# Attention of a hybrid encoder layer as a fixed-order pipeline, with the merge gates ahead of it and the softmax division moved to the outputs

## The chip, the cores and the metric

One core of one Trainium2 chip. The metric is the device time of one execution in microseconds, the median of several runs. The core has a matmul engine (PE, with its weight loads PEld), a vector engine (DVE), a scalar engine (ACT), a general engine (POOL, GpSimd) and a sequencer that issues most DMAs (SP). Each of them takes its instructions in the order in which they stand in its queue; they wait for each other through semaphores.

## The reference, cut to what matters

One layer is applied to two independent groups of 512 tokens (prompt and sample) with the same weights, all in float32. The part that is changed is latent attention with 8 heads, and the sigmoid merge gates that weigh both branches later.

```python
scale = (A_NOPE + A_ROPE) ** -0.5                       # (128 + 64) ** -0.5
qa = (rmsnorm(c_q, g_q) @ w_uq).reshape(B, S, A_HEADS, A_NOPE + A_ROPE)
q_nope, q_rope = qa[..., :A_NOPE], rope(qa[..., A_NOPE:], cos, sin)
kv = (rmsnorm(c_kv, g_kv) @ w_ukv).reshape(B, S, A_HEADS, A_NOPE + A_V)
k_nope, va = kv[..., :A_NOPE], kv[..., A_NOPE:]
k_rope = rope(k_r, cos, sin)                            # one key for all heads
s = q_nope . k_nope + q_rope . k_rope                   # per head, 512 x 512
p = softmax(s * scale)
y_a = (p @ va) @ w_ao
g_m, g_a = split(sigmoid(gm))                           # the merge gates, gm = h @ w
x = x + (g_m * y_m + g_a * y_a) @ w_out
```

## The kernel before

Tokens lie along the free axis, 512 to a tile (`T`), features along the 128 partitions; `g` is the group. A float32 product is made of three reduced-precision products: each operand is split into a high half (a cast to `float32r`, by ACT) and a low half (source minus high, `lo_of`, L153, by DVE, or by POOL for the values), and PE multiplies high by high, low by high and high by low. `split` (L156), `weight` (L163) and `proj1` (L175) do this for activations, weights and a projection.

The stages are: normalisation, the mLSTM heads with their chain, the merge gates, latent attention, two output projections by a scheme of seven products (`chain` and `Seven`), the last projection, the feed-forward part and an embedding. Around the change:

- `lat_norms` (L650) scales the latent vectors of q and kv by their inverse root mean squares.
- `merge_gate` (L684) projects one block of 128 gate channels for both groups: 48 matmuls, then a product and a tanh, and a store to DRAM. There are 16; `BULK` (L1426) says how many stand ahead of the value projection (10), after the first head's projections (2), and after heads 0 to 3 (1 each).
- The values of all heads are projected at L708 to L723 and stored to DRAM (`vd`).
- `attn_proj` (L762) makes the operands of one half-head, a head for one group: for even heads the rotary part of q for two heads (`rope`, L730, which reads the projection's bank in PSUM and shifts 32-partition blocks), then q and k, then loads the values and splits them.
- `attn` (L780) does, for each of four blocks of 128 queries: five score matmuls into a bank `sc`; row maximum (DVE, L794) and its negative times the scale; the exponential with the row sum (ACT, L797); the reciprocal; the rescaling of the probabilities `p` (ACT L800, or DVE L802 for block 1); four transposes on PE (L805) into a bank `pt`; the high half `aph` (ACT, L807) and the low half `apl` (DVE, L808). Then twelve matmuls weigh the values (L812 to L814), and the output goes to DRAM (`ozd`).
- `hops.need` (L867) prepares operands of the next stage (named P1, P2, P7, P6; P7 and P6 need a subtraction, on DVE and POOL), two or three after each half-head of heads 4 to 6 (`HOPS`, L1424).

What is not pinned is ordered by a planner, which simulates a timeline and can put instructions of one part between those of another; `pinned` (L65) makes all following instructions of DVE, ACT, PE and POOL, POOL's DMA issues included, keep the order of the program on their engine. In attention nothing is pinned. Banks in PSUM: two `pj`, three `sc`, two `pt`, one `av`.

Of the kernel before, what the change touches and what calls it, by code (L numbers as in the profile page):

```python
# [7 lines left out]
F32 = mybir.dt.float32  # L8
# [7 lines left out]
P = 128  # L16
# [46 lines left out]
def encoder_kernel(ctx: ExitStack, tc: tile.TileContext, a):  # L63
# [666 lines left out]
    def rope(src, nblk, by_dma=False):  # L730
        n = 32 * nblk
        r = Q("tr", "rp")
        V.tensor_tensor(out=r[0:n], in0=src[0:n], in1=cos[0:n], op=ALU.mult)
        s = Q("tr", "rs")
        m = EV("ch", "rm") if by_dma else None
        if by_dma:
            V.tensor_tensor(out=m, in0=src, in1=sin, op=ALU.mult)
        for i in range(nblk):
            f, o = slice(32 * i, 32 * i + 32), slice(32 * (i ^ 1), 32 * (i ^ 1) + 32)
            if by_dma:  # L740
                nc.sync.dma_start(s[o], m[f])
            else:
                V.tensor_tensor(out=s[o], in0=src[f], in1=sin[f], op=ALU.mult)
        V.tensor_tensor(out=r[0:n], in0=r[0:n], in1=s[0:n], op=ALU.add)
        return r

    kst = []
    for g in range(G):
        gs = Q("tr", "gs")
        nc.sync.dma_start(gs[0:64], gsd[g])  # L750
        r = rope(gs, 2)
        kh = Q.pool.tile([P, T], F32R, name=f"kh{g}")
        kl = Q.pool.tile([P, T], F32R, name=f"kl{g}")
        for o in (0, 64):
            S.copy(kh[o : o + 64], r[0:64])
        for o in (0, 64):
            V.tensor_tensor(out=kl[o : o + 64], in0=r[0:64], in1=kh[0:64].bitcast(F32), op=ALU.subtract)
        kst.append((kh, kl))
    scale = (128 + 64) ** -0.5
    qst = [[None] * 2 for _ in range(G)]  # L760

    def attn_proj(hd, g, wa):  # L762
        if hd % 2 == 0:
            r = rope(proj1(wa, lat["cq"][g], 2, 0, "pj"), 4, hd == 0)
            st0 = Q("qst", "qs0", F32R)
            st1 = Q("qst", "qs1", F32R)
            S.copy(st0[0:64], r[0:64])
            S.copy(st1[64:128], r[64:128])
            V.tensor_tensor(out=st0[64:128], in0=r[0:64], in1=st0[0:64].bitcast(F32), op=ALU.subtract)
            V.tensor_tensor(out=st1[0:64], in0=r[64:128], in1=st1[64:128].bitcast(F32), op=ALU.subtract)  # L770
            qst[g] = [st0, st1]
        qn = split(proj1(wa, lat["cq"][g], 2, 256, "pj"), Q, "qkv", "qn")
        kn = split(proj1(wa, lat["ckv"][g], 2, 512, "pj"), Q, "qkv", "kn")
        vt = Q("tr", "avt")
        c = hd % 4 * P
        nc.sync.dma_start(vt.rearrange("p (a b) -> p a b", a=NB), vd[g][hd // 4].rearrange("a p c -> p a c")[:, :, c : c + P])
        vn = split(vt, Q, "qkv", "vn", GP)
        return qn, kn, vn, qst[g][hd % 2]

    def attn(hd, g, ops):  # L780
        (qh, ql), (nh, nl), (vh, vl), q2 = ops
        kh, kl = kst[g]
        ph = Q("ph", "aph", F32R, (P, NB, T))
        pl = Q("pl", "apl", F32R, (P, NB, T))
        for i in range(NB):
            c = slice(i * P, (i + 1) * P)
            bk = bank("sc")
            E.matmul(bk, qh[:, c], nh, start=True, stop=False)
            E.matmul(bk, qh[:, c], nl, start=False, stop=False)
            E.matmul(bk, ql[:, c], nh, start=False, stop=False)  # L790
            E.matmul(bk, q2[:, c], kh, start=False, stop=False)
            E.matmul(bk, q2[:, c], kl, start=False, stop=True)
            mx = sm.tile([P, 4], F32, name=nm("mx"), tag="mx", bufs=4)
            V.tensor_reduce(out=mx[:, 0:1], in_=bk, axis=mybir.AxisListType.X, op=ALU.max)  # L794
            V.tensor_scalar(out=mx[:, 1:2], in0=mx[:, 0:1], scalar1=-scale, scalar2=None, op0=ALU.mult)
            p = Q("p", "p")
            S.activation(out=p, in_=bk, func=AF.Exp, bias=mx[:, 1:2], scale=scale, accum_out=mx[:, 2:3])  # L797
            V.reciprocal(out=mx[:, 3:4], in_=mx[:, 2:3])
            if i != 1:
                S.activation(out=p, in_=p, func=AF.Copy, scale=mx[:, 3:4])  # L800
            else:
                V.tensor_scalar(out=p, in0=p, scalar1=mx[:, 3:4], scalar2=None, op0=ALU.mult)  # L802
            tp = bank("pt")
            for j in range(NB):
                E.transpose(tp[:, j * P : (j + 1) * P], p[:, j * P : (j + 1) * P], ident)  # L805
            tp3 = tp.rearrange("p (a b) -> p a b", a=NB)
            S.copy(ph[:, :, c], tp3)  # L807
            lo_of(pl[:, :, c], tp3, ph[:, :, c])  # L808
        ob = bank("av")
# [227 lines left out]
    wa = weight(a["wa"][0])  # L1037
    ops = [attn_proj(0, g, wa) for g in range(G)]
    for _ in range(BULK[1]):
        merge_gate(*bulk.pop(0))  # L1040
    for hd in range(AH):
        if hd < AH - 1:
            wa = weight(a["wa"][hd + 1])
        else:
            QL.close()
            X2 = Slots("X2", "right", x=16)
            assert not units
            hops.r, hops.t = {}, {}
            hops.raw = lambda g, k: load(hzd[g][k], X2, "x")
        for g in range(G):  # L1050
            attn(hd, g, ops[g])
            if hd < AH - 1:
                ops[g] = attn_proj(hd + 1, g, wa)
            for _ in range(HOPS.get((hd, g), 0)):
                hops.need(*units.pop(0))
        for _ in range(BULK[2 + hd]):
            merge_gate(*bulk.pop(0))
# [461 lines left out]
```

## Time and profile before

| | us |
|---|---|
| median of 3 runs | 1871.39 (1870.98 to 1872.51) |
| the profiled execution | 1872.55 |
| its span | 1870.8 |
| merge gates and value projection, from about 484 to 561 | 77 |
| attention, from about 561 to 848 | 287 |

Durations come from the profiled execution; the span is from its first to its last instruction, and 1.75 us lie around it. Times in a view are from the span's start. A name such as `apl<-pt,aph` means that tile `apl` is written from `pt` and `aph`; buffer numbers are left out.

### The profile page before, as it was taken

The page shows a single profiled execution, that of the slowest core. Times are in us where ns is not written, and L with a number is a line of the kernel's source. Part 1 is how long each engine was busy: PE and PEld are TensorE (multiplying, and loading weights), DVE is VectorE, ACT ScalarE, POOL GpSimd, SP SyncE. Part 2 cuts the span into 40 slices and gives each one's busy share as a digit, 9 for nine tenths or more (in the row PEclk, how much of TensorE's full clock was granted, in tenths as well). Part 3 has the DMA queues.
Part 4 walks back from the last instruction along what each step waited for, and adds up shares of the span by engine and source line. Part 5 has one row for each costly group of instructions (what it writes and reads, how often), then busy time and mean ns, then how long its engine had stood idle before and what let it go on. Part 6 is the DMA issues. An engine that isn't in the chain of part 4 may idle for free.

```text
span 1870.8 us, 24407 instructions
## 1 busy us (share of the span) xinstructions
PE 1831.6 (98%) x8801; PEld 1524.5 (81%) x8801; DVE 1244.1 (67%) x2196; ACT 890.1 (48%) x1725; POOL 385.8 (21%) x281
## 2 busy tenths in 40 slices
PE   9999999999999999899999999999999999999997
PEld 7889898988887888678878888887888877888786
DVE  6767575767616757976997586444444469878656
ACT  6255555653334656784543364333333343534333
POOL 0101010100000001241230005654666423111000
PEclk9999999999999999999999999999999999999998
DMA  4211212122443113345564332322233256533332
GB/s 166 66 57 52 67 47 79 35 74 79 141 155 107 65 63 117 109 146 210 181 205 155 117 141 74 124 96 96 91 106 119 96 169 209 168 126 103 105 130 96
DMA packets 100617, 212.40 MB, mean 114 GB/s; under 512 B 10960, under 2 KB 21584, under 8 KB 100496
## 3 DMA queue, kind: packets, MB, share of 16 engines
q1 hardware_dynamic: 87840, 166.01, 26.2%
q10 hardware_dynamic: 12096, 43.00, 6.8%
q8 instruction: 69, 1.13, 0.2%
q0 software_dynamic: 560, 1.84, 0.2%
q14 instruction: 52, 0.43, 0.1%
HBM read 156.05 MB, written 54.23 MB: 112 GB/s over the span
## 4 chain that ended last, share of the span: by engine, by line
PE 84%; DVE 9%; DMA 3%; ACT 2%; issue 1%; SPq 0%; ACTq 0%; DVEq 0%
PE b L945 12%; PE b L947 12%; PE b L946 12%; PE mm L183 8%; PE mm L185 8%; PE mm L184 8%; PE mm L79 3%; PE nm L622 3%; DVE xl L154 2%; PE mm L542 2%; PE mm L541 2%; PE mm L540 2%; DVE wp L154 1%; PE pt L805 1%; PE mm L1311 1%
## 5 line engine op out<-in xcount | busy, mean ns | idle before, releaser
L946 PE MATMUL b<-xl,wp 128*128 128x512 f32 x1148 | 448.3, 392 | 1.8 <-DVE xl L154 1.8
L945 PE MATMUL b<-xh,wp 128*128 128x512 f32 x1148 | 442.1, 393 | 6.9 <-ACT u L986 2.3
L947 PE MATMUL b<-xh,wp 128*128 128x512 f32 x1148 | 444.0, 392 | 1.8 <-DVE wp L154 1.8
L889 ACT CAST wp<-wst 128x512 fp32r<-128x512 f32 (+1 forms) x270 | 164.3, 612 | 307.4 <-PE b L947 259.9
L154 DVE TENSOR_TENSOR wp<-wst,wp 128x512 fp32r<-128x512 f32 (+1 forms) x270 | 234.3, 870 | 65.8 <-ACT wp L889 65.7
L945 PEld LDWEIGHTS b<-xh,wp 128*128 128x128 f32 x1148 | 216.0, 188 | 59.6 <-ACT wp L889 5.7
L947 PEld LDWEIGHTS b<-xh,wp 128*128 128x128 f32 x1148 | 216.0, 188 | 49.7 <-DVE wp L154 2.7
L946 PEld LDWEIGHTS b<-xl,wp 128*128 128x128 f32 x1148 | 215.9, 188 | 49.1 <-DVE xl L154 2.7
L183 PE MATMUL mm<-hh,whi 128*128 128x512 f32 x560 | 219.7, 392 | 0.2 <-DVE qnl L154 0.2
L184 PE MATMUL mm<-hl,whi 128*128 128x512 f32 x560 | 218.6, 390 | 0.0
L185 PE MATMUL mm<-hh,wlo 128*128 128x512 f32 x560 | 218.5, 391 | 0.0
L991 DVE TENSOR_TENSOR u<-b,u 128x512 f32<-128x512 f32 x90 | 61.6, 688 | 132.4 <-PE b L947 82.6
L185 PEld LDWEIGHTS mm<-hh,wlo 128*128 128x128 f32 x560 | 105.2, 188 | 21.9 <-DVE wlo L154 0.3
L183 PEld LDWEIGHTS mm<-hh,whi 128*128 128x128 f32 x560 | 105.2, 188 | 21.7 <-DVE qnl L154 0.7
L168 ACT CAST whi<-wst 128x1024 fp32r<-128x1024 f32 (+1 forms) x69 | 70.7, 1025 | 108.5 <-PE mm L184 67.7
L184 PEld LDWEIGHTS mm<-hl,whi 128*128 128x128 f32 x560 | 105.2, 188 | 21.0
L916 POOL TENSOR_TENSOR s<-wst,wst 128x512 f32<-128x512 f32 (+1 forms) x30 | 48.2, 1606 | 323.3 <-DMA wst<-w 148.0
L154 DVE TENSOR_TENSOR wlo<-wst,whi 128x1024 fp32r<-128x1024 f32 (+1 forms) x69 | 83.9, 1216 | 34.6 <-ACT whi L168 33.8
L986 ACT COPY u<-b 128x512 f32<-128x512 f32 x90 | 50.8, 589 | 97.8 <-PE b L947 72.2
L1209 POOL TENSOR_TENSOR sg<-sg,u 128x512 f32<-128x512 f32 x30 | 55.0, 1833 | 203.6 <-DVE u L991 203.6
L154 DVE TENSOR_TENSOR xl<-ld,xh 128x512 fp32r<-128x512 f32 x121 | 90.0, 771 | 5.6 <-ACT xh L873 4.9
L154 POOL TENSOR_TENSOR vnl<-avt,vnh 128x512 fp32r<-128x512 f32 x16 | 21.2, 1322 | 344.1 <-ACT vnh L158 285.7
(346 smaller groups left out, 3601.1 us busy)
## 6 DMA issues: line engine op xcount, KB each, us to landing
wst<-w SPq DMA_DIRECT2D x73, 512.0 KB, 3.3
wst<-w ACTq DMA_DIRECT2D x60, 512.0 KB, 3.4
ld<-actd SPq DMA_DIRECT2D x77, 256.0 KB, 3.9
actd<-t SPq DMA_DIRECT2D x40, 256.0 KB, 3.0
x<-x SPq DMA_DIRECT2D x32, 256.0 KB, 4.7
ld<-hzd SPq DMA_DIRECT2D x32, 256.0 KB, 2.8
wst<-wd ACTq DMA_DIRECT2D x16, 512.0 KB, 3.5
actd<-sg SPq DMA_DIRECT2D x30, 256.0 KB, 2.1
```

What stands on the lines that cost most here:

```text
L79: r = f(*args, **kw)
L154: e.tensor_tensor(out=out, in0=src, in1=hi.bitcast(F32), op=ALU.subtract)
L168: S.copy(hi[:, :n], st[:, :n])
L183: E.matmul(bk, whi[:, c], hi, start=k == 0, stop=False)
L184: E.matmul(bk, whi[:, c], lo, start=False, stop=False)
L185: last_mm[0] = E.matmul(bk, wlo[:, c], hi, start=False, stop=k == nk - 1)
L622: E.matmul(bk, l, r, start=n == 0, stop=n == len(terms) - 1)
L889: S.copy(hi, src)
L945: E.matmul(bk, whi[:, c], hi, start=bool(first) and k == 0, stop=False, **sk)
L946: E.matmul(bk, whi[:, c], lo, start=False, stop=False, **sk)
L947: E.matmul(bk, wlo[:, c], hi, start=False, stop=k == self.kh - 1, **sk)
L991: V.tensor_tensor(out=t, in0=b, in1=t, op=ALU.add if name == "P2" else ALU.subtract)
```

## The change

All 16 merge gates stand ahead of the value projection (`BULK = [16]`). The scale of the scores goes into q's normalisation. Attention becomes a loop over `u`, the 16 half-heads, pinned from its first to its last instruction, in which the steps of half-head `u`, of the one before and of the one after are written in one order; `m` is `u // 4` (two heads, both groups) and `r` is `u % 4`. The probabilities stay undivided. The reciprocals of the row sums are transposed, stored to DRAM and loaded back as a row on all partitions (both DMAs issued by POOL), and POOL multiplies the output by that row. The rotary steps work on a copy of the projection in SBUF (tag `rt` in `AX`) and are spread over several half-heads, as are the splits of the weights. `WX`, the weight tiles of the next stage, is opened after half-head 12. The scores' matmul with q's low half comes last of its five. The products with the probabilities' low halves come last of the twelve.

```diff
@@ lat_norms
-            V.tensor_tensor(out=r[:, c], in0=r[:, c], in1=rcol[g], op=ALU.mult)
+            V.scalar_tensor_tensor(
+                out=r[:, c], in0=r[:, c], scalar=SCALE if n == "cq" else 1.0, in1=rcol[g], op0=ALU.mult, op1=ALU.mult
+            )
@@ tiles
-    Q = Slots("Q", tr=3, qkv=12, qst=4, p=3, ph=1, pl=1)
+    Q = Slots("Q", vt=2, rb=1, qkv=12, qst=4, p=3, ph=1, pl=1)
-    WX = Slots("WX", "right", wst=2, s3=2, wp=1)
+    AX = Slots("AX", "right", rt=4)
@@ new functions in place of rope, attn_proj and attn
+    def rope_steps(t, s, nblk):
+        n = 32 * nblk
+        for i in range(nblk):
+            f, o = slice(32 * i, 32 * i + 32), slice(32 * (i ^ 1), 32 * (i ^ 1) + 32)
+            yield V.tensor_tensor(out=s[o], in0=t[f], in1=sin[f], op=ALU.mult)
+        yield V.tensor_tensor(out=t[0:n], in0=t[0:n], in1=cos[0:n], op=ALU.mult)
+        yield V.tensor_tensor(out=t[0:n], in0=t[0:n], in1=s[0:n], op=ALU.add)
...
+    def wa_split(hd):
+        w = was[hd] = [WP(n, n, F32R, (P, 1024)) for n in ("whi", "wlo")]
+        st = wload[hd]
+        for c in (slice(256, 768), slice(0, 256)):
+            if c.start == 256 or hd in (0, 1, 3, 5):
+                S.copy(w[0][:, c], st[:, c])
+                lo_of(w[1][:, c], st[:, c], w[0][:, c])
+    def rot_proj(m, g):
+        t = rots[m, g] = AX("rt", "rp")
+        S.copy(t, proj1(was[max(2 * m - 1, 0)], lat["cq"][g], 2, 0, "pj"))
+        rsteps[m, g] = rope_steps(t, AX("rt", "rs"), 4)
...
+    def score(u, i):
...
+        E.matmul(bk, qn[u][0][:, c], kn[u][0], start=True, stop=False)
+        E.matmul(bk, qn[u][0][:, c], kn[u][1], start=False, stop=False)
+        E.matmul(bk, q2[:, c], kst[g][0], start=False, stop=False)
+        E.matmul(bk, q2[:, c], kst[g][1], start=False, stop=False)
+        E.matmul(bk, qn[u][1][:, c], kn[u][0], start=False, stop=True)
+        V.tensor_reduce(out=x["mx"][:, i : i + 1], in_=bk, axis=mybir.AxisListType.X, op=ALU.max, negate=True)
...
+    def sums_row(u):
...
+        E.transpose(tp[0:NB, 0:P], x["rc"], ident)
+        rb = x["rb"] = Q("rb", "rb")
+        S.copy(rb[0:NB, 0:P], tp[0:NB, 0:P])
+        GP.dma_start(rsd[g][hd], rb[0:NB, 0:P])
+        GP.dma_start(rb, rsd[g][hd].rearrange("a p -> (a p)")[None, :].to_broadcast([P, T]))
...
+    def weighed(u):
...
+        S.copy(o, x["ob"])
+        GP.tensor_tensor(out=o, in0=o, in1=x["rb"], op=ALU.mult)
         nc.sync.dma_start(ozd[g][hd], o)
@@ the loop, in place of that over heads and groups
+    def hop_hi(n, k):
+        src = hops.part(n, k)
+        hi, lo = op(n, "xh", F32R), op(n, "xl", F32R)
+        S.copy(hi, src)
...
+    pinned[0] = True
+    for u in range(NU + 1):
+        now, then, nxt = u < NU, u > 0, u + 1 < NU
+        m, r = u // 4, u % 4
+        if now:
+            score(u, 0)
+            expo(u, 0)
+            score(u, 1)
...
+        if then:
+            turn(u - 1, 3)
+        if now:
+            expo(u, 1)
+        if then:
+            V.reciprocal(out=att[u - 1]["rc"], in_=att[u - 1]["den"])
+            turn_lo(u - 1, 3)
+        if nxt:
+            proj_hi(kn, u + 1, "ckv", 512)
+            proj_lo(kn, u + 1)
+        if now:
+            vn[u] = [Q("qkv", n, F32R) for n in ("vh", "vl")]
+            S.copy(vn[u][0], vts[u])
+            lo_of(vn[u][1], vts[u], vn[u][0], GP)
+        if then:
+            sums_row(u - 1)
+        los = []
+        if now and r:
+            for n in (("P1", "P2"), ("P7",), ("P6",))[r - 1]:
+                los.append(hop_hi(n, m))
...
+        if r == 0 and 0 < m < 4:
+            rot_hi(m, 1)
+            rot_lo(m, 1)
+        if m < 3:
+            if r == 0:
+                rot(m + 1, 0, 2)
+            if r == 1:
+                rot(m + 1, 0, 4)
+            if r == 2:
+                rot(m + 1, 1, 4)
+            if r == 3:
+                rot(m + 1, 1, 2)
+                rot_hi(m + 1, 0)
+                rot_lo(m + 1, 0)
+        if then:
+            weigh(u - 1)
+            weighed(u - 1)
+        if now:
+            turn(u, 0)
+            turn_lo(u, 0)
+            score(u, 2)
+            turn(u, 1)
+            expo(u, 2)
+            turn_lo(u, 1)
+        if r == 1 and m < 3:
+            wa_split(2 * m + 2)
+        if r == 3 and m < 3:
+            wa_split(2 * m + 3)
+        for x in los:
+            lo_of(*x)
+        if nxt:
+            proj_hi(qn, u + 1, "cq", 256)
+        if now:
+            score(u, 3)
+        if nxt:
+            proj_lo(qn, u + 1)
+        if now:
+            turn(u, 2)
+            expo(u, 3)
+            turn_lo(u, 2)
+        if r == 0 and m < 3:
+            rot_proj(m + 1, 1)
+        if r == 3 and m < 2:
+            rot_proj(m + 2, 0)
...
-BULK = [10, 2, 1, 1, 1, 1, 0, 0, 0, 0]
+BULK = [16]
```

`turn` transposes one block of probabilities and casts the high half, `turn_lo` makes the low half; `rot` runs some of the rotary steps, `rot_hi` and `rot_lo` split their result; `proj_hi` and `proj_lo` project and split k or q; `weigh` is the twelve value matmuls.

More of the change, by code (lines that the diff above doesn't have):

```diff
@@ L724, in encoder_kernel @@
     ozd = [[dr.tile([P, T], F32, name=f"ozd{g}_{c}") for c in range(AH)] for g in range(G)]
+    rsd = [[dr.tile([NB, P], F32, name=f"rsd{g}_{c}") for c in range(AH)] for g in range(G)]
     cos = Q.pool.tile([P, T], F32, name="cos")
@@ L728, in encoder_kernel @@
     nc.sync.dma_start(sin, a["sin"])
-    def rope(src, nblk, by_dma=False):
+    def rope_steps(t, s, nblk):
         n = 32 * nblk
[L732 to L737, printed above, removed]
         for i in range(nblk):
             f, o = slice(32 * i, 32 * i + 32), slice(32 * (i ^ 1), 32 * (i ^ 1) + 32)
[L740 to L745, printed above, removed]
+            yield V.tensor_tensor(out=s[o], in0=t[f], in1=sin[f], op=ALU.mult)
+        yield V.tensor_tensor(out=t[0:n], in0=t[0:n], in1=cos[0:n], op=ALU.mult)
+        yield V.tensor_tensor(out=t[0:n], in0=t[0:n], in1=s[0:n], op=ALU.add)
     kst = []
     for g in range(G):
-        gs = Q("tr", "gs")
+        gs = AX("rt", "gs")
         nc.sync.dma_start(gs[0:64], gsd[g])
-        r = rope(gs, 2)
+        for _ in rope_steps(gs, AX("rt", "rs"), 2):
+            pass
         kh = Q.pool.tile([P, T], F32R, name=f"kh{g}")
@@ L754, in encoder_kernel @@
         for o in (0, 64):
-            S.copy(kh[o : o + 64], r[0:64])
+            S.copy(kh[o : o + 64], gs[0:64])
         for o in (0, 64):
-            V.tensor_tensor(out=kl[o : o + 64], in0=r[0:64], in1=kh[0:64].bitcast(F32), op=ALU.subtract)
+            V.tensor_tensor(out=kl[o : o + 64], in0=gs[0:64], in1=kh[0:64].bitcast(F32), op=ALU.subtract)
         kst.append((kh, kl))
[L759 to L774, printed above, removed]
+    halves_ = [(hd, g) for hd in range(AH) for g in range(G)]
@@ new lines, in encoder_kernel, with wa_load @@
+    NU = len(halves_)
+    was, wload, qn, kn, vn, vts, rots, rsteps, qst, att = ({} for _ in range(10))
+    def wa_load(hd):
+        wload[hd] = WP("wst", "wst", F32, (P, 1024))
+        nc.sync.dma_start(wload[hd][:, 0:768], a["wa"][hd])
+    def wa_split(hd):
[5 more added lines that the diff above has]
+                lo_of(w[1][:, c], st[:, c], w[0][:, c])
@@ new lines, in rot_proj, with rot, rot_hi @@
+    def rot_proj(m, g):
+        t = rots[m, g] = AX("rt", "rp")
+        S.copy(t, proj1(was[max(2 * m - 1, 0)], lat["cq"][g], 2, 0, "pj"))
+        rsteps[m, g] = rope_steps(t, AX("rt", "rs"), 4)
+    def rot(m, g, n):
+        for _ in range(n):
+            next(rsteps[m, g])
+    def rot_hi(m, g):
+        t = rots[m, g]
+        qst[m, g] = st = [Q("qst", "qs", F32R) for _ in range(2)]
+        for i in range(2):
+            f = slice(64 * i, 64 * i + 64)
+            S.copy(st[i][f], t[f])
@@ new lines, in rot_lo, with proj_hi, proj_lo @@
+    def rot_lo(m, g):
+        t, st = rots[m, g], qst[m, g]
+        for i in range(2):
+            f, o = slice(64 * i, 64 * i + 64), slice(64 - 64 * i, 128 - 64 * i)
+            V.tensor_tensor(out=st[i][o], in0=t[f], in1=st[i][f].bitcast(F32), op=ALU.subtract)
+    def proj_hi(to, u, n, off):
+        hd, g = halves_[u]
+        bk = proj1(was[hd], lat[n][g], 2, off, "pj")
+        hi = Q("qkv", "qh", F32R)
+        S.copy(hi, bk)
+        to[u] = (hi, Q("qkv", "ql", F32R), bk)
+    def proj_lo(to, u):
+        hi, lo, bk = to[u]
+        lo_of(lo, bk, hi)
@@ L775, in attn_proj, with v_load @@
+    def v_load(u):
+        hd, g = halves_[u]
+        vt = vts[u] = Q("vt", "avt")
         c = hd % 4 * P
         nc.sync.dma_start(vt.rearrange("p (a b) -> p a b", a=NB), vd[g][hd // 4].rearrange("a p c -> p a c")[:, :, c : c + P])
[L777 to L809, printed above, removed]
@@ new lines, in score @@
+    def score(u, i):
+        hd, g = halves_[u]
+        if i == 0:
+            att[u] = dict(
+                mx=sm.tile([P, NB], F32, name=nm("mx"), tag="mx", bufs=2),
+                den=sm.tile([P, NB], F32, name=nm("den"), tag="den", bufs=2),
+                rc=sm.tile([P, NB], F32, name=nm("rc4"), tag="rc4", bufs=1),
+                bk={}, p={}, tp={},
+            )
+        x, c, q2 = att[u], slice(i * P, (i + 1) * P), qst[hd // 2, g][hd % 2]
+        bk = x["bk"][i] = bank("sc")
+        E.matmul(bk, qn[u][0][:, c], kn[u][0], start=True, stop=False)
[4 more added lines that the diff above has]
+        V.tensor_reduce(out=x["mx"][:, i : i + 1], in_=bk, axis=mybir.AxisListType.X, op=ALU.max, negate=True)
@@ new lines, in expo, with turn @@
+    def expo(u, i):
+        x = att[u]
+        p = x["p"][i] = Q("p", "p")
+        S.activation(
+            out=p, in_=x["bk"][i], func=AF.Exp, bias=x["mx"][:, i : i + 1], accum_out=x["den"][:, i : i + 1]
+        )
+    def turn(u, i):
+        x = att[u]
+        if i == 0:
+            x["ph"] = Q("ph", "aph", F32R, (P, NB, T))
+            x["pl"] = Q("pl", "apl", F32R, (P, NB, T))
+        tp = bank("pt")
+        for j in range(NB):
+            E.transpose(tp[:, j * P : (j + 1) * P], x["p"][i][:, j * P : (j + 1) * P], ident)
+        x["tp"][i] = tp.rearrange("p (a b) -> p a b", a=NB)
+        S.copy(x["ph"][:, :, i * P : (i + 1) * P], x["tp"][i])
@@ L810, in attn, with weigh @@
+    def weigh(u):
+        x, (vh, vl) = att[u], vn[u]
+        ob = x["ob"] = bank("av")
         for j in range(NB):
             c = slice(j * P, (j + 1) * P)
-            E.matmul(ob, vh[:, c], ph[:, j], start=j == 0, stop=False)
-            E.matmul(ob, vl[:, c], ph[:, j], start=False, stop=False)
-            E.matmul(ob, vh[:, c], pl[:, j], start=False, stop=j == NB - 1)
+            E.matmul(ob, vh[:, c], x["ph"][:, j], start=j == 0, stop=False)
+            E.matmul(ob, vl[:, c], x["ph"][:, j], start=False, stop=False)
+        for j in range(NB):
+            E.matmul(ob, vh[:, j * P : (j + 1) * P], x["pl"][:, j], start=False, stop=j == NB - 1)
@@ L815, in attn @@
+    def weighed(u):
+        hd, g = halves_[u]
+        x = att[u]
         o = EV("ch", "oz")
-        S.copy(o, ob)
+        S.copy(o, x["ob"])
+        GP.tensor_tensor(out=o, in0=o, in1=x["rb"], op=ALU.mult)
         nc.sync.dma_start(ozd[g][hd], o)
@@ L1018, in encoder_kernel @@
     hops.tmp = lambda: None
-    units = [(n, [k]) for k in range(4) for n in ("P1", "P2", "P7", "P6")]
     z1d = [[dr.tile([P, T], F32, name=f"z1d{g}_{c}") for c in range(KD)] for g in range(G)]
@@ L1035, in pair @@
         return ops, lambda: Seven(srcs, 4, ops, outputs(put), e)
[L1037 to L1044, printed above, removed]
+    for hd in range(2):
+        wa_load(hd)
+        wa_split(hd)
+    v_load(0)
+    for g in range(G):
+        rot_proj(0, g)
+        rot(0, g, 6)
+        rot_hi(0, g)
+        rot_lo(0, g)
@@ new lines, in encoder_kernel, with hop_load @@
+    for to, n, off in ((kn, "ckv", 512), (qn, "cq", 256)):
+        proj_hi(to, 0, n, off)
+        proj_lo(to, 0)
+    rot_proj(1, 0)
+    def hop_load(k):
+        for x in "acbd":
+            hops.get(x, k)
+    def hop_hi(n, k):
+        src = hops.part(n, k)
+        hi, lo = op(n, "xh", F32R), op(n, "xl", F32R)
+        S.copy(hi, src)
+        hops.x.setdefault(n, []).append((hi, lo))
+        return lo, src, hi
+    hop_load(0)
+    pinned[0] = True
[7 more added lines that the diff above has]
+        if nxt:
+            v_load(u + 1)
+            if r == 0 and m < 3:
+                wa_load(2 * m + 2)
+            if r == 2 and m < 3:
+                wa_load(2 * m + 3)
+        if then:
[19 more added lines that the diff above has]
+            if r == 3 and m < 3:
+                hop_load(m + 1)
+        if r == 0 and 0 < m < 4:
[24 more added lines that the diff above has]
+            wa_split(2 * m + 2)
+        if r == 3 and m < 3:
+            wa_split(2 * m + 3)
[5 more added lines that the diff above has]
+            score(u, 3)
+        if nxt:
+            proj_lo(qn, u + 1)
[3 more added lines that the diff above has]
+            turn_lo(u, 2)
+        if r == 0 and m < 3:
+            rot_proj(m + 1, 1)
+        if r == 3 and m < 2:
+            rot_proj(m + 2, 0)
+        if u == 12:
+            AX.close()
+            WX = Slots("WX", "right", wst=2, s3=2, wp=1)
+        if u == NU - 2:
@@ L1045, in encoder_kernel @@
             QL.close()
             X2 = Slots("X2", "right", x=16)
[L1047 to L1057, printed above, removed]
+    pinned[0] = False
@@ L1058, in encoder_kernel @@
+    hops.r, hops.t = {}, {}
+    hops.raw = lambda g, k: load(hzd[g][k], X2, "x")
     assert not bulk
@@ L1467, in _layout @@
     for hd in range(AH):
-        wa[hd, :, 0:256] = rq[hd // 2]
+        wa[hd, :, 0:256] = rq[min((hd + 1) // 2, AH // 2 - 1)]
         wa[hd, :, 256:512] = uq[hd]
```

8 lines of the change are left out of this document (7 added, 1 removed).

## The prediction, made before the changed kernel ran

> **What bounds the kernel now.** The page first, for who is busy; then windows, to see where that breaks down.
>
> ```profile
> span 1870.8 us, 24407 instructions
> ...
> PE 1831.6 (98%) x8801; PEld 1524.5 (81%) x8801; DVE 1244.1 (67%) x2196; ACT 890.1 (48%) x1725; POOL 385.8 (21%) x281
> ```
>
> PE is busy 98%, but the ends of matmuls are modelled, so I count instructions instead. Windows of all instructions, windows of those on `pt` alone (the transposes), and a line of the chain that ended last:
>
> ```profile
> 484.00:557.00 73.00, 73.00 (x327) 60.39 (x326) 29.64 (x40) 27.11 (x42) 0.00 (x0) 1.00 0.47 160
> ...
> 557.00:736.00 179.00, 178.42 (x845) 146.51 (x845) 113.98 (x228) 103.42 (x200) 12.11 (x9) 1.00 0.26 85
> 736.00:848.00 112.00, 101.31 (x483) 79.54 (x482) 88.99 (x186) 83.44 (x174) 39.18 (x30) 0.98 0.40 128
> ...
> 557.00:736.00 179.00, 18.83 (x128) 15.69 (x128) 21.80 (x32) 18.58 (x32) 1.00 0.26 85
> 736.00:848.00 112.00, 19.52 (x128) 15.52 (x128) 21.95 (x32) 19.12 (x32) 0.98 0.40 128
> ...
> 597.42 0.87 PE pt L805 x8
> ```
>
> Columns of a window: its length, then busy time and count of PE, PEld, DVE, ACT, POOL, then PE's granted clock. From 484 to 557 gates and v projection issue 319 matmuls and 8 transposes without a gap: a transpose takes 0.87 / 8 = 0.109 us, a 512-wide matmul (73.0 - 0.87) / 319 = 0.226. At that rate 557 to 736 needs 717 x 0.226 + 128 x 0.109 = 176.0 of its 179.0, and 736 to 848 needs 355 x 0.226 + 14.0 = 94.2 of 112.0. Attention loses 3.0 us while merge gates (48 matmuls, 10.9 us each) fill it, and 17.8 without them: **20.8 us is all that a better order can win here**, and elsewhere nothing is touched.
>
> **The change part by part.** *Gates.* Six move ahead of attention, 65 us there instead of here, at the full rate of 484 to 557, where DVE (29.6 of 73) and ACT (27.1) leave them room: price 0. What goes is the filler.
>
> *Small parts.* Sixteen transposes of the sums: 16 x 0.109 = 1.7 us more PE. In `lat_norms` one instruction becomes another: 0. Weights and values are loaded by SP a unit ahead: 0, and a late load would cost at most its landing. The next stage's weight tiles (WX) exist only from the 13th unit on; three units, some 36 us, remain to load them: 0.
>
> *The pipeline.* With 16 half-heads ("units") and no filler, all depends on whether four in-order engines keep step. The durations:
>
> ```profile
> 598.65 0.69 ACT L797 ACTIVATE p<-sc,mx 128x512 f32<-128x512 f32 x1
> 599.24 0.20 ACT L797 ACTIVATION_READ_ACCUMULATOR p<-sc,mx 128x1 f32 x1
> 599.33 0.63 ACT L688 ACTIVATE tg<-tg 128x512 f32<-128x512 f32 x1
> 599.85 0.59 ACT L807 CAST aph<-pt 128x512 fp32r<-128x512 f32 x1
> 600.32 0.61 ACT L158 CAST qnh<-pj 128x512 fp32r<-128x512 f32 x1
> ...
> 574.09 1.28 DVE L794 TENSOR_REDUCE mx<-sc 128x1 f32<-128x512 f32 x2
> ...
> 570.95 0.69 DVE L769 TENSOR_TENSOR qs<-rp,qs 64x512 fp32r<-64x512 f32 x1
> 571.67 1.78 DVE L770 TENSOR_TENSOR qs<-rp,qs 64x512 fp32r<-64x512 f32 x1
> ...
> 571.61 1.30 POOL L154 TENSOR_TENSOR vnl<-avt,vnh 128x512 fp32r<-128x512 f32 x1 [158.20 <-ACT vnh L158]
> ...
> 763.00 0.68 DVE L743 TENSOR_TENSOR rs<-pj,sin 32x512 f32<-32x512 f32 x1
> 763.71 0.69 DVE L154 TENSOR_TENSOR apl<-pt,aph 128x512 fp32r<-128x512 f32 x1
> ...
> 763.23 1.29 POOL L917 TENSOR_TENSOR wst<-wst 128x512 f32<-128x512 f32 x1
> ```
>
> From start to start: an exponential 0.68, a copy from PSUM 0.47 (from SBUF I take 0.52); a DVE instruction 1.28 - 0.68 = 0.60, one that shifts partitions (`qs`, rotary) 0.71. And a coupling: `qs` at 571.67 takes two SBUF tiles and needs 1.78, ending 0.5 after POOL's `vnl` ends at 572.9, while `rs` and `apl`, which read PSUM, run at 0.68 beside POOL's add at 763.23. So a DVE instruction on two SBUF tiles waits for POOL's. Before, the rotary products read `pj` in PSUM; now they read its copy in SBUF, behind kn's low half, just when POOL splits the values: 1.3 us lost in most units.
>
> Need per unit on PE: 20 score, 12 projection, 12 value matmuls and 17 transposes, 11.84 us; with a rotary projection 13.2. By these rates DVE needs 8.9 to 10.5 and ACT 8 to 9, so no engine but PE is full. The loss comes from the order. I walk it from the start of a unit's first score, with 0.06 us from a release to a start and 0.2 for a weight load that was held.
>
> **Second unit of a group of four.** DVE: two maxima to 3.2, low half of the last probabilities 4.3 (after ACT's copy), kn's 5.6, four rotary instructions from 6.8 (behind POOL) to 9.5, two low halves and a maximum to 11.4. Then the weights' low half, which waits for ACT's high half (after the third exponential) until 12.3; two low halves of the next stage's operands (P1, P2) to 14.1; only then the fourth maximum, 14.7, and q's low half, 15.3. PE wants that for the fifth matmul of the next unit's first score at about 13.2: late by 2.3, and the third unit's third exponential makes PE's T2 late by about 1 more. The third unit of a group so loses 3.5, three times.
>
> **Fourth unit.** POOL's order is: values, store of the sums' reciprocals to DRAM, broadcast load back, P6's subtraction, product. The load must wait for the store's landing on POOL's own queue, and behind it stands P6; ACT waits for P6, and behind that on ACT stand the rotary copies, the output's copy, two probability copies and the third exponential, for which PE waits. Prices of a store from POOL:
>
> ```profile
> 1563.05 0.54 POOL L1220 DMA_DIRECT2D actd<-t  x1 [1.26 <-DVE t L1216]
> ...
> actd<-sg SPq DMA_DIRECT2D x6, 256.0 KB, 2.0
> ...
> actd<-sg POOLq DMA_DIRECT2D x3, 256.0 KB, 4.6
> ...
> 59.64 2.36 DMA lfd<-lf
> ...
> DMA to landing us min/median/max: 3.2/3.4/3.6
> ```
>
> A 256 KB store from POOL lands after 4.6, from SP 2.0; a small one from SP (`lfd`) 2.36. This small one from POOL lies between 2.0 and 4.6; I take 3.0, nearer to `lfd` by size. The broadcast (16 such by SP, `b<-nmd`, 3.4) holds only the product behind it. Sum: values end 7.0, store landed 10.0, load issued 10.6, P6 done 11.9, ACT's copy 12.0 instead of 5.9; then 0.52 + 2 x 0.52 + 3 x 0.48, the third maximum, the exponential, and PE's T2 starts at 17.1 instead of 11.7: 5.4, of which 2.0 to 4.6 for the landing makes 4.4 to 7.0. Behind T2 the rotary projection waits 1.2 for its weights, split after that exponential. So 6.8, 6.8, 5.7, 6.9 in the four groups.
>
> [...]
>
> *Ends.* First unit 2.3 (no previous unit's work between its scores and its transposes); second units 0.5 each, last group's third 0.4, first units 0.6, 0.6, 1.7; draining the last unit 2.7. Head: from split weights to the first score the chain is projection 1.4, copy 0.6, six rotary instructions 4.1, copies 1.1, low halves 1.4, in all 8.6 with hops, against 30 projection matmuls (6.8 us), of which some wait too: I take 3, between 0 and 6.
>
> **Sum.** Third units 10.9, fourth 26.2, first ones 2.3 + 2.9, second 1.9, drain 2.7: 46.9 lost, and 3 ahead. Against the old loss: -20.8 + 1.7 + 46.9 + 3 = +30.8. The profiled execution took 1872.55 (span and 1.8 around it), so 1903.4; it lies 1.2 above the median, so **1902**.
>
> **The rivals.** *ACT isn't held by the store* (lands early, or P6's copy has slack behind it): walking with P6 on DVE, the fourth units lose 14 less in all, 1888. Against it: even 2.0 us of landing leaves 4.4.
>
> *Nor does DVE wait for POOL:* walked without both, the units lose 16.4 instead of 46.9, 1872. Against it: the 1.78 row. Together with the next one this is the only way to no change.
>
> *Faster: PE stays full.* 48 rescalings go from ACT, at 0.74, and 16 from DVE:
>
> ```profile
> L800 ACT ACTIVATE p<-p,mx 128x512 f32<-128x512 f32 x48 | 34.5, 736 | 16.1 <-DVE mx L798 15.6 <-DVE mx L795 0.5
> ```
>
> That is 2.2 us of ACT per unit, and idle waits of 16.1 that vanish with it. If it makes the third exponential end before T2's turn in every unit, only first unit, drain and head (8 us) remain: -20.8 + 1.7 + 8 = -11, 1860. It decides at T2: ACT may be held by no more than about 1 us at P6.
>
> *Slower still.* The store lands after 4.6 (+10 by the walk), and PE's clock falls:
>
> ```profile
> 770.00:790.00 20.00, 16.26 (x69) 12.55 (x69) 19.71 (x40) 14.87 (x30) 2.59 (x2) 0.91 0.43 126
> ```
>
> After gaps of 2 us near 770 the granted clock of this window is 0.91, 1.8 us of half speed. Four gaps of 5.4 could each cost about 1.8: +7. Either or both, 1909 to 1919. [...]
>
> **How the numbers follow.** Forecast 0.45 (1893 to 1908), ACT not held 0.17, neither wait 0.10, PE full 0.17, slower still 0.11. The range leaves out part of the lowest and of the highest: 1863 to 1914. What a measurement of this kernel can tell from no change is about 0.2%, 3.7 us. Same 0.07, from the third case; faster 0.18; slower 0.75.
>
> **What would show it.** Right: in every fourth unit ACT's `xh` waits some 6 us for POOL's subtraction, itself behind a DMA; PE idles 4 to 7 us before a transpose; rotary instructions on DVE show 1.8 us beside `vnl`; the gates' stretch is 65 us longer at full rate. Wrong: P6's copy waits under 1 us, or attention's 16 units take under 13 us each. The forecast fails if the order lets ACT run ahead where I have it stand behind P6.

## The result, and the profile after

| | median, us | runs |
|---|---|---|
| before, all four runs | 1871.18 | 1869.65 to 1872.51 |
| after | 1921.28 | 1919.33 to 1923.67 |
| ratio | 1.0269 | 95% interval 1.0251 to 1.0286 |

The changed kernel is slower by 50.1 us, where 30.8 were forecast and the range ended at 1914. The side was right, the size was not. The profiled execution took 1919.33. (Medians here and below are of fast executions; the only slow one, among the ten of the division alone, took 4143 us and is left out.)

The page of after first: its span, the busy time of each engine, and the granted clock in forty slices.

```profile
span 1917.5 us, 24414 instructions
...
PE 1843.9 (96%) x8817; PEld 1528.6 (80%) x8817; DVE 1240.7 (65%) x2078; ACT 870.7 (45%) x1705; POOL 423.5 (22%) x329
...
PEclk9999999999999999998999999999999999999998
```

PE carries out 16 instructions more, DVE 118 fewer, ACT 20 fewer, POOL 48 more. DVE and ACT have less work than before, and still the span is longer: the time went to waiting. Windows by stage say where (length, then busy time and count of PE, PEld, DVE, ACT, POOL, then the granted clock):

```profile
484.00:627.00 143.00, 143.00 (x634) 117.89 (x633) 45.24 (x59) 42.79 (x64) 0.00 (x0) 1.00 0.39 130
627.00:639.00 12.00, 8.71 (x33) 6.50 (x32) 10.51 (x17) 4.72 (x9) 0.00 (x0) 0.83 0.38 122
639.00:896.00 257.00, 212.87 (x995) 165.58 (x994) 172.29 (x259) 144.41 (x319) 87.11 (x85) 0.93 0.30 96
```

Gates and value projection run without a gap and end 66 us later than before, as they should. From 639 to 896 lies the loop. Its 995 instructions, 272 of them transposes, need 723 x 0.226 + 272 x 0.109 = 193.0 at full rate, so 64.0 are lost in the loop, where 46.9 were forecast; in the head, 627 to 639, 33 x 0.226 = 7.5 of 12.0 are needed and 4.5 lost, where I had 3. Waits in the loop, in total, number and longest:

```profile
POOL rb L79 <- DMA rsd<-rb: 38.9, 14, 4.5
...
PE pt L79 <- ACT p L79: 36.6, 10, 14.5
ACT xh L79 <- POOL ld L79: 36.2, 4, 15.7
```

Read from the bottom: four times ACT's `xh` (P6) waits for POOL's subtraction, ten times PE's transposes wait for ACT's exponential, and POOL itself waits for the store of the sums. (L79 is the line of the function that pins.) The timeline of POOL, ACT and PE in the first fourth unit shows how they hang together:

```profile
686.13 0.56 POOL L79 DMA_DIRECT2D rsd<-rb  x1
689.44 0.57 POOL L79 DMA_DIRECT2D rb<-rsd  x1 [2.74 <-DMA rsd<-rb]
690.02 1.30 POOL L79 TENSOR_TENSOR ld<-ld,ld 128x512 f32<-128x512 f32 x1
...
691.36 0.62 ACT L79 CAST xh<-ld 128x512 fp32r<-128x512 f32 x1 [6.38 <-POOL ld L79]
...
690.73 0.39 PE L79 MATMUL sc<-qh,ql 128*128 128x512 f32 x1
696.42 1.12 PE L79 MATMUL pt<-ident,p 128*128 128x128 f32 x4 [5.30 <-ACT p L79]
```

POOL stands 2.74 us with the load at the head of its queue until the store has landed; behind it stands a subtraction that needs neither. ACT stands 6.38 for that, and PE 5.30. The four groups' gaps, from start to start and less the instruction itself, are 5.5, 6.8, 5.5 and 14.7 us. The 6.8 is the unit in which POOL waited 4.11 for its landing. The last one has a further cause, in POOL's, ACT's and PE's timelines there:

```profile
868.40 2.52 POOL L916 TENSOR_TENSOR ld<-ld,ld 128x512 f32<-128x512 f32 x2
870.89 1.28 POOL L79 TENSOR_TENSOR vl<-avt,vh 128x512 fp32r<-128x512 f32 x1
872.13 0.56 POOL L79 DMA_DIRECT2D rsd<-rb  x1
872.70 1.29 POOL L916 TENSOR_TENSOR ld<-ld,ld 128x512 f32<-128x512 f32 x1
873.94 3.69 POOL L922 TENSOR_TENSOR ld<-ld,ld 128x512 f32<-128x512 f32 x3
877.60 1.25 POOL L923 TENSOR_TENSOR ld<-ld,ld 128x512 f32<-128x512 f32 x1
878.82 1.25 POOL L922 TENSOR_TENSOR ld<-ld,ld 128x512 f32<-128x512 f32 x1
880.04 2.47 POOL L923 TENSOR_TENSOR ld<-ld,ld 128x512 f32<-128x512 f32 x2
882.46 0.58 POOL L79 DMA_DIRECT2D rb<-rsd  x1
883.06 1.27 POOL L79 TENSOR_TENSOR ld<-ld,ld 128x512 f32<-128x512 f32 x1
...
884.37 0.62 ACT L79 CAST xh<-ld 128x512 fp32r<-128x512 f32 x1 [15.68 <-POOL ld L79]
...
888.14 1.12 PE L79 MATMUL pt<-ident,p 128*128 128x128 f32 x4 [14.49 <-ACT p L79]
```

Lines 916, 922 and 923 are sums of the next stage's operands. They aren't pinned, so the planner put eight of them, from 872.70 to 882.5, between two pinned instructions: into the wait for the landing. They take 9.8 us, the landings of the other units about 3. Two more stand ahead of the values' subtraction (`vl`), which starts 2.3 us after ACT has its operand ready, at 868.6.

The third mark is the clock. Two windows behind fourth units' gaps:

```profile
696.40:699.80 3.40, 3.38 (x10) 2.74 (x11) 2.90 (x6) 2.39 (x6) 0.00 (x0) 0.51 0.30 84
...
888.00:894.00 6.00, 4.04 (x13) 2.85 (x14) 2.63 (x5) 2.09 (x7) 0.56 (x1) 0.50 0.41 136
```

PE restarts at half the clock, granted 0.51 and 0.50. In the first row four transposes and six matmuls, 1.8 us at full rate, take 3.4. Stretches of half clock begin at 635, 696, 758, 819 and 877 and last 6.8, 3.4, 6.8, 6.8 and 17.1 us; before, there was one of 3.4 in attention, at 773.9, granted 0.50. Start to start, and without the waits between them, PE's instructions in them take 2.7 + 1.7 + 2.6 + 2.4 + 1.8 = 11.2 us more than at full rate. What sets the lengths of the stretches isn't shown.

### The profile page after: what moved, and what is told of

It reads as the page before. It is cut to its first block, busy times and chain, and to the rows that moved or that the text cites. A ratio compares the mean times of both kernels' runs of the same rounds, so it can differ in the third digit from the quotient of the medians.

```text
span 1917.5 us, 24414 instructions
## 1 busy us (share of the span) xinstructions
PE 1843.9 (96%) x8817; PEld 1528.6 (80%) x8817; DVE 1240.7 (65%) x2078; ACT 870.7 (45%) x1705; POOL 423.5 (22%) x329
## 4 chain that ended last, share of the span: by engine, by line
PE 81%; DVE 10%; DMA 3%; ACT 3%; issue 2%; POOL 1%; SPq 0%; ACTq 0%; DVEq 0%; POOLq 0%
PE b L1004 12%; PE b L1006 12%; PE b L1005 12%; PE mm L183 8%; PE mm L185 8%; PE mm L184 8%; PE mm L79 3%; PE nm L622 3%; PE sc L79 2%; PE pj L79 2%; PE mm L542 2%; PE mm L541 2%; PE mm L540 2%; DVE xl L154 1%; PE pt L79 1%
## 5 line engine op out<-in xcount | busy, mean ns | idle before, releaser
L168 ACT CAST whi<-wst 128x1024 fp32r<-128x1024 f32 x61 | 64.1, 1051 | 109.5 <-PE mm L184 70.4
L154 DVE TENSOR_TENSOR wlo<-wst,whi 128x1024 fp32r<-128x1024 f32 (+1 forms) x65 | 77.7, 1198 | 34.5 <-ACT whi L768 19.6
L79 POOL TENSOR_TENSOR vl<-avt,vh 128x512 fp32r<-128x512 f32 x16 | 21.1, 1320 | 307.5 <-ACT vh L79 307.5
L154 DVE TENSOR_TENSOR xl<-ld,xh 128x512 fp32r<-128x512 f32 x105 | 79.2, 785 | 5.0 <-ACT xh L932 4.4
```

The costliest lines, as they stand in the source:

```text
L79: r = f(*args, **kw)
L154: e.tensor_tensor(out=out, in0=src, in1=hi.bitcast(F32), op=ALU.subtract)
L168: S.copy(hi[:, :n], st[:, :n])
```

## The experiments

My theory after this reading: of the 50 us some 30 come from ACT standing behind P6 in four fourth units, 9 of them from the foreign sums in the last; the clock adds what the gaps cost on top. Rivals: the subtraction on POOL is slow in itself; the gates' absence costs it all; the new operations, not their order, do.

### P6's subtraction on DVE

```diff
-    hops = Ops(hraw, None, lambda n: V if n == "P7" else GP)
+    hops = Ops(hraw, None, lambda n: V if n in ("P7", "P6") else GP)
```

> P6's subtraction goes from POOL to DVE, nothing else. Theory (ACT stands behind P6, P6 on POOL behind the wait for the stored reciprocals): PE's gaps before T2 in the fourth half-head of each group (5.7, 7.0, 5.8 and 14.9 us in the changed kernel) fall under 1.5 us, PE's clock stays full in attention, and the loop from first score to last value product falls from 257 to about 227 us, so the time to about 1890. Rival (the gaps come from the order on DVE and the missing filler, POOL only coincides): gaps over 4 us stay and the time stays over 1912.

Measured 1901.55, ratio 1.0166 (1.0151 to 1.0181). The first three of these gaps fall to 0.9 us each. The last one stays, at 12.5, though nothing of P6 is left on POOL. DVE's and POOL's timelines there say why:

```profile
856.94 11.62 DVE L79 TENSOR_TENSOR xl<-ld,xh 128x512 fp32r<-128x512 f32 x1
868.48 0.68 DVE L79 TENSOR_REDUCE mx<-sc 128x1 f32<-128x512 f32 x1
...
856.37 1.29 POOL L916 TENSOR_TENSOR ld<-ld,ld 128x512 f32<-128x512 f32 x1
857.61 3.69 POOL L922 TENSOR_TENSOR ld<-ld,ld 128x512 f32<-128x512 f32 x3
861.27 1.25 POOL L923 TENSOR_TENSOR ld<-ld,ld 128x512 f32<-128x512 f32 x1
862.49 1.25 POOL L922 TENSOR_TENSOR ld<-ld,ld 128x512 f32<-128x512 f32 x1
863.71 2.47 POOL L923 TENSOR_TENSOR ld<-ld,ld 128x512 f32<-128x512 f32 x2
866.13 0.58 POOL L79 DMA_DIRECT2D rb<-rsd  x1
866.73 1.27 POOL L923 TENSOR_TENSOR ld<-ld,ld 128x512 f32<-128x512 f32 x1
```

A subtraction of two SBUF tiles, 0.69 us elsewhere, starts on DVE and lasts 11.62: it ends 0.6 us after the last of POOL's sums (nine from 856.37 on, and the issue of the load), and the maximum that PE's transposes hang on stands behind it. So taking P6 off POOL's queue gives back 20 us, not 30: the run of sums holds the last unit by this second way also.

### The row of sums by SP, P6 still on POOL

```diff
-        GP.dma_start(rsd[g][hd], rb[0:NB, 0:P])
-        GP.dma_start(rb, rsd[g][hd].rearrange("a p -> (a p)")[None, :].to_broadcast([P, T]))
+        nc.sync.dma_start(rsd[g][hd], rb[0:NB, 0:P])
+        nc.sync.dma_start(rb, rsd[g][hd].rearrange("a p -> (a p)")[None, :].to_broadcast([P, T]))
```

> Both DMAs of the reciprocals' row are issued by SP instead of POOL; P6 stays on POOL. Theory (the wait on POOL's queue is the cost, not the subtraction): P6 runs right behind the values' split, ACT is held 1 to 2 us, the gaps before T2 fall under 2 us and the time to 1888 to 1896. Rival (POOL's subtraction itself is too slow or in the wrong place): gaps and time as in the changed kernel, 1921. A second rival: SP's queue now waits for the store, loads of values come late, and ACT waits for them: over 1900.

Measured 1901.67, 1.0170 (1.0153 to 1.0187), the same as with P6 on DVE. One wait of its loop:

```profile
ACT xh L79 <- POOL ld L79: 13.7, 4, 4.8
```

36.2 us have become 13.7, with the same subtraction on the same engine. The place in POOL's queue behind a DMA's landing is what costs, not the subtraction; that rival is out. The other rival, that SP's queue now brings the values late, expected over 1900 and so has the right number, but not its cause: no wait of ACT for a load stands in the loop. The gaps before T2 are 2.0, 2.0, 2.0 and 3.8. It lies 6 us above the upper end of what I expected: the values' subtraction and P6's stand in a row on POOL (1.28 and 1.74 us in the first fourth unit), and ACT still waits for the second.

### The next stage's sums on DVE

```diff
     hops.raw = lambda g, k: load(hzd[g][k], X2, "x")
+    hops.sums = lambda n: V
```

> The sums of the next stage's operands (P5, Q4), which the planner puts on POOL between the store and the load back in the last group, go to DVE. Theory (eight foreign instructions of 1.25 us ahead of P6 make the last gap 14.9 instead of 5.7): the last gap falls to 5 to 7 us, the others stay, PE's slow clock there is shorter; 1906 to 1911. Rival (the last gap has another cause, such as the end of the loop): gap over 12 us and 1918 or more.

Measured 1916.22, 1.0243 (1.0228 to 1.0258): 5 us instead of the 10 to 15. The last gap falls from 14.7 to 6.4, the other three stay (5.4, 6.7, 5.5). POOL's timeline has the reason for the rest:

```profile
872.12 0.56 POOL L79 DMA_DIRECT2D rsd<-rb  x1
877.73 0.57 POOL L79 DMA_DIRECT2D rb<-rsd  x1 [5.04 <-DMA rsd<-rb]
```

With the sums gone, a landing of 5.04 us holds the queue by itself. And a gap of 2.8 stands before a transpose at 869, where after had 0.7.

### The gates alone, on the kernel before

```diff
-BULK = [10, 2, 1, 1, 1, 1, 0, 0, 0, 0]
+BULK = [16, 0, 0, 0, 0, 0, 0, 0, 0, 0]
```

> The kernel before with all 16 gates ahead of the value projection and nothing else of the change. Theory (the gates were the filler that hid attention's waits): attention loses about 2 us per half-head instead of 0.4 in the first eight, 10 to 16 us in all, 1881 to 1887. Rival (the planner keeps PE full there without gates, and the first half-heads carry no operands of the next stage): within 4 us of 1871.

Measured 1879.59, 1.0050 (1.0035 to 1.0065): 9.6 us, just under the 10 to 16 that I expected. Attention in its windows:

```profile
635.00:856.00 221.00, 205.60 (x988) 162.65 (x987) 180.46 (x387) 164.31 (x343) 51.72 (x39) 0.99 0.28 92
```

988 instructions, some 256 of them transposes, need about 193.3, so 28 us are lost without filler, where before lost 20.8. The filler's absence costs a fifth of the 50 us, not most of them.

### The values' split at the unit's start

To P6 on DVE this adds: the split of the values (ACT's copy and POOL's subtraction) stands at the start of the unit and no longer beside the rotary instructions.

```diff
         if now:
+            vn[u] = [Q("qkv", n, F32R) for n in ("vh", "vl")]
+            S.copy(vn[u][0], vts[u])
+            lo_of(vn[u][1], vts[u], vn[u][0], GP)
+        if now:
             score(u, 0)
...
             proj_lo(kn, u + 1)
-        if now:
-            vn[u] = [Q("qkv", n, F32R) for n in ("vh", "vl")]
-            S.copy(vn[u][0], vts[u])
-            lo_of(vn[u][1], vts[u], vn[u][0], GP)
```

> As e1 (P6 on DVE, 1901.6), and each half-head's values are split at its start, where DVE works on PSUM, instead of ahead of the rotary steps. Theory (DVE's instructions on two SBUF tiles wait while POOL works): rotary instructions fall from 1.7 to 0.7 us, the third half-heads' waits for q's low half (1.6) go, and the time falls by about 11 us to 1890. Rival (the third half-heads wait for the sheer number of DVE instructions): within 3 us of e1.

Measured 1897.71, 1.0144 (1.0128 to 1.0159): 3.8 us less, where I expected 11. The groups of DVE show that the coupling is real; first the kernel with P6 on DVE, then this one:

```profile
L79 DVE TENSOR_TENSOR rs<-rp,sin 32x512 f32<-32x512 f32 x24 | 21.3, 886 | 0.5
```

```profile
L79 DVE TENSOR_TENSOR rs<-rp,sin 32x512 f32<-32x512 f32 x24 | 16.4, 683 | 0.4
```

The rotary instructions lose their 0.2 us each. But POOL's product of the outputs now falls beside other instructions of DVE on two SBUF tiles, in the timelines of DVE and POOL:

```profile
660.64 2.38 DVE L79 TENSOR_TENSOR xl<-ld,xh 128x512 fp32r<-128x512 f32 x2
...
660.37 1.50 POOL L79 TENSOR_TENSOR oz<-oz,rb 128x512 f32<-128x512 f32 x1 [3.21 <-DMA rb<-rsd]
```

Two instructions that take 1.29 together in after (at 664.61) take 2.38 here, ahead of the same maximum and the same low half of q. The third units' wait for that low half is still 2.4, 2.3 and 1.3 us. The coupling was moved.

### Both: the values early, and the next stage's sums on DVE

```diff
     hops.raw = lambda g, k: load(hzd[g][k], X2, "x")
+    hops.sums = lambda n: V
```

> As e5, and the next stage's sums (P5, Q4) go from POOL to DVE. In e1 one DVE instruction lasts 11.6 us beside a run of POOL's sums. Theory (POOL's run of instructions holds DVE as long as it lasts): the 11.6 us instruction and the gap of 12.5 us of PE go, 9 to 12 us less than e5 in the time. Rival (the last half-head is late for another reason): no more than 3 us less.

Measured 1887.06, 1.0086 (1.0071 to 1.0102): 10.6 less than without this line, as the theory had it. No instruction of DVE is stretched to 10 us any more. So the run of foreign sums on POOL is worth 10.6 us here, where P6 is on DVE.

### The next operands' low halves behind q's

To that, one step of DVE is moved:

```diff
-        for x in los:
-            lo_of(*x)
         if nxt:
             proj_hi(qn, u + 1, "cq", 256)
         if now:
             score(u, 3)
         if nxt:
             proj_lo(qn, u + 1)
+        for x in los:
+            lo_of(*x)
```

> As e8, and the low halves of the next stage's operands come after q's low half on DVE, not ahead of the fourth maximum. Theory (PE waits for q's low half): 2 us less than e8. Rival: no change, as only the place of the wait moves.

Measured 1888.19, 1.0087 (1.0070 to 1.0103): no difference. The third units' waits of 2.4 and 2.2 us for q's low half are gone, and others came before transposes, 1.8 at 775 and 4.4 at 855 in place of 2.5 there.

### The division alone, on the kernel before

The probabilities aren't rescaled; the row of reciprocals goes through DRAM by SP, and POOL multiplies the output. Nothing is pinned, and the gates stay where they were.

```diff
-            V.reciprocal(out=mx[:, 3:4], in_=mx[:, 2:3])
-            if i != 1:
-                S.activation(out=p, in_=p, func=AF.Copy, scale=mx[:, 3:4])
-            else:
-                V.tensor_scalar(out=p, in0=p, scalar1=mx[:, 3:4], scalar2=None, op0=ALU.mult)
...
+        V.reciprocal(out=den, in_=den)
+        tr_ = bank("pt")
+        E.transpose(tr_[0:NB, 0:P], den, ident)
+        rb = EV("bk", "rb")
+        S.copy(rb[0:NB, 0:P], tr_[0:NB, 0:P])
+        nc.sync.dma_start(rsd[g][hd], rb[0:NB, 0:P])
+        nc.sync.dma_start(rb, rsd[g][hd].rearrange("a p -> (a p)")[None, :].to_broadcast([P, T]))
...
+        GP.tensor_tensor(out=o, in0=o, in1=rb, op=ALU.mult)
```

> The kernel before with the division alone: probabilities not rescaled, the reciprocals' row over DRAM by SP, the product by POOL; gates, order and planner as before. Theory (ACT's waits for the reciprocals and 34.5 us of rescaling stood behind part of the 17.8 us lost in the last eight half-heads): 3 to 8 us faster than before, 1863 to 1867. Rival (these waits are covered, or the row's way over DRAM and POOL's product take their place): within 3 us of 1870 or slower.

Measured 1872.55, 1.0011 (1.0001 to 1.0020): no gain; the theory failed and its rival holds. Its windows:

```profile
557.00:736.00 179.00, 177.70 (x842) 144.67 (x841) 106.52 (x193) 89.37 (x184) 20.70 (x16) 1.00 0.29 94
736.00:848.00 112.00, 102.23 (x494) 80.86 (x493) 84.83 (x155) 69.25 (x154) 51.34 (x38) 0.98 0.45 149
```

Against before ACT is busy 14.1 us less in each window, and PE isn't held any less: with 136 transposes to a window it needs 174.4 of 179 and 95.7 of 112, so 20.9 us are lost, where before lost 20.8. PE's waits for ACT's exponentials fell only from 4.6 to 3.6 us, and 1.6 us of waits ahead of the new transposes of the reciprocals came in. What the missing rescalings alone would give isn't separated here from what the row costs; together they give nothing.

### The changed kernel in the planner's order

```diff
     hop_load(0)
-    pinned[0] = True
     for u in range(NU + 1):
```

> The changed kernel with the loop's order left to the planner: every operation of the change, none of its fixed order. The planner puts the first groups' P6 on POOL ahead of the stores. Theory (the order is what costs; the operations themselves cost little): 1877 to 1890, near the kernel before with all gates ahead (1879.6). Rival (the row's way over DRAM and the rotary steps in SBUF cost in any order): 1900 or more.

Measured 1887.82, 1.0099 (1.0084 to 1.0114). All of the change is in it but the fixed order, and 33.5 of the 50 us are gone. POOL's timeline around a store of the sums:

```profile
681.86 1.34 POOL L154 TENSOR_TENSOR vl<-avt,vh 128x512 fp32r<-128x512 f32 x1 [0.36 <-ACT vh L1146]
683.15 0.56 POOL L857 DMA_DIRECT2D rsd<-rb  x1
686.44 0.58 POOL L858 DMA_DIRECT2D rb<-rsd  x1 [2.72 <-DMA rsd<-rb]
690.34 1.28 POOL L875 TENSOR_TENSOR oz<-oz,rb 128x512 f32<-128x512 f32 x1 [3.32 <-DMA rb<-rsd]
692.08 1.29 POOL L154 TENSOR_TENSOR vl<-avt,vh 128x512 fp32r<-128x512 f32 x1 [0.47 <-ACT vh L1146]
694.05 1.28 POOL L913 TENSOR_TENSOR ld<-ld,ld 128x512 f32<-128x512 f32 x1 [0.68 <-POOL vl L154]
```

POOL waits for the landing as long as in the fixed order (2.72). But the subtraction (line 913) stands elsewhere, and ACT's `xh` waits for POOL once in its loop, for 0.3 us. So what a wait on POOL's queue cost depended here on what stood behind it: ACT's waits for that subtraction sum to 36.2 us in the fixed order and to 0.3 in this one.

### The repaired order without pinning

The same edit on the kernel with the values early and the sums on DVE.

> As e8 (P6 and the next stage's sums on DVE, values split early), with the order left to the planner. Theory (with POOL's waits gone, what is left of the fixed order's cost is about the 7.5 us by which e8 stands over the gates alone): 1876 to 1883. Rival (e8's rest has nothing to do with the order): within 3 us of e8's 1887.

Measured 1884.92, 1.0079 (1.0062 to 1.0096): 2.1 less than pinned. That is above the 1883 at which the theory ended; the rival, within 3 us of 1887, holds. Once the two faults are out, the fixed order costs next to nothing, and it wins nothing.

No version beats the kernel before.

## Why the prediction was right in its side and wrong in its size

| from | to | us |
|---|---|---|
| before | gates ahead, alone | +9.6 |
| gates ahead | all operations of the change, planner's order | +8.2 |
| planner's order | fixed order: the change | +33.5 |
| the change | P6 off POOL's queue | -19.7 |
| that | values' split early | -3.8 |
| that | next stage's sums off POOL | -10.6 |

The last three take the fixed order to 1887.1, against the planner's 1887.8. So two faults of the order, P6 behind the store and the foreign sums, make 30 of the 50 us. (The first line is against 1869.99, the median of before on that chip; the others are differences of medians. The runs were made on several chips; with each taken against before on its own chip, the lines shift by up to 1.2 us.)

**What bounds it, and the filler.** Right. 20.8 us was all that could be won, and moving the gates wins none of it: alone it loses 9.6. The gates' stretch is longer by their 65 us at full clock (1.00 in its window).

**Fourth unit.** The mechanism was right in each link: store, load, subtraction, ACT's copy, transposes. Its size was near for three groups: 5.4 forecast, 5.5, 6.8 and 5.5 found. The store's landing, taken as 3.0, has this row in the DMA view of the loop:

```profile
rsd<-rb POOLq DMA_DIRECT2D x16, 2.0 KB, 2.8
```

The 1.2 us for the rotary projection didn't appear: in the 696 unit it starts 0.8 us after the first of the four transposes, which take that long at half clock.

**The step that failed** is the price of the *last* fourth unit, which I put at 6.9 in all, 5.4 of it the gap, by POOL's order of the loop alone. The next stage was thought of once, for its weight tiles, at "0". Its sums stand on POOL's queue as well: the values' subtraction starts 2.3 us late, and P6 starts 12.2 us after it, where 5.1 were enough in the first fourth unit. The gap is 14.7 instead of 5.4, 9.3 too long. That the sums are the cause is shown by the run that moves them alone: the gap falls by 8.3, to 6.4. The time falls by 5.1 only; a gap of 2.8 came in elsewhere. With P6 on DVE, where the same run stretched one instruction of DVE, 10.6 us of the time came back.

**The clock** is the second step: it was in the text, but as a rival at 0.11 and not as a term. By the prediction's own estimate, about 1.8 us for a gap of 5.4, from a clock of 0.91 after gaps of 2, it belonged to the forecast, once for each of the four gaps expected there. Behind the gaps of 5.30 and 14.49 the clock measured 0.51 and 0.50. Priced there at 7, it measured 8.5 in the four fourth units and 2.7 at the head and the first scores, where I had priced none. By the windows, head and loop lost 68.5 where 49.9 were forecast, 18.6 more. The last unit is 7.8 of it, against its 6.9, and the clock 11.2; the rest are small terms of both signs. (The two profiled executions are 46.8 apart, 16.0 over the forecast, so these shares are good to some 3 us.)

**Third units** measured 0.5 + 1.6 before the score and 0.7 before T2, 2.8 instead of 3.5, thrice. DVE's wait for POOL was as forecast, here on the first of two rotary instructions:

```profile
657.61 2.38 DVE L79 TENSOR_TENSOR rs<-rp,sin 32x512 f32<-32x512 f32 x2
...
657.46 1.29 POOL L79 TENSOR_TENSOR vl<-avt,vh 128x512 fp32r<-128x512 f32 x1 [10.81 <-ACT vh L79]
```

With it gone from the rotary instructions only 3.8 us came back, since DVE then waited for POOL elsewhere. So the rival's 1872, in which DVE never waits, was not reached, and no run here shows what it would give.

**Ends.** First unit 1.6 (2.3 forecast), drain 1.7 + 0.8 (2.7), head 4.5 (3, between 0 and 6), 1.4 of it the half clock that is counted above.

**The rivals.** "ACT isn't held" was rightly the exception: taking the hold away made 1901.6, though, and not the 1888 of my walk, since the run of sums held the same unit by DVE. "PE stays full" falls: with the rescalings gone and the row of reciprocals in their place, all else as before, PE lost as much as before. "Slower still" ended at 1919 and came nearest, but its landing of 4.6 measured 2.8, and its clock of 7 was too small, so that it came near is luck. (That landing would give four times 1.6 by the interval of 4.4 to 7.0, not the 10 of the text. A unit's need on PE sums to 11.80, not 11.84; nothing hangs on it.)

**Open.** The changed operations in the planner's order cost 8.2 us beyond the gates, and 7.5 of it stay in the best fixed order. The division alone costs 2 to 3; how the rest divides among the rotary copies, the order of the products and the splits wasn't tried.

## What to carry to other kernels

When a DMA that waits for another DMA is put on an engine's queue, list what stands behind it on that queue and who needs it; here some 3 us of landing became 5 us of PE and more, four times, and moving either the DMAs or the bystander gave 20 us back. A part pinned by hand isn't closed as long as others may place instructions on the same engine: the price of its last step is read with the next stage's work on the queue. And gaps of several microseconds on PE are priced with the half clock behind them, here 8.5 us behind four.

## What the runs showed of the hardware that was not expected

An instruction of DVE on two SBUF tiles lasted in two kernels not as long as one instruction of POOL beside it but as long as a whole run of them: 11.62 us beside sums that end at 868.0, and 10.59 at the same place in the kernel with the values early, against 0.69 alone. It isn't always so. With the row of sums by SP the same instruction of DVE got in between two of these sums:

```profile
868.11 0.76 DVE L79 TENSOR_TENSOR xl<-ld,xh 128x512 fp32r<-128x512 f32 x1
...
865.83 5.39 POOL L922 TENSOR_TENSOR ld<-ld,ld 128x512 f32<-128x512 f32 x4
```

It took 0.76, and POOL's four sums 5.39, where three took 3.69 above and a fourth adds 1.25. What decides between the two isn't shown. In the two long waits DVE did not get done between one instruction of POOL and the next, not even during the 0.58 us of a DMA issue, at 866.13 in the first.

The landing of the same 2 KB store from POOL varied much: 2.7 us of waiting in one unit, 5.04 in another kernel's last.
